# Four projections by seven block products, their weight sums begun at the split of the input, copies on SyncE's queue

## The chip, the core and the metric

The kernel runs on one core of a Trainium2 chip. A core has four compute engines and a fifth that only issues transfers, each with its own instruction queue: TensorE (PE, matrix products into an accumulator memory, PSUM), VectorE (DVE), ScalarE (ACT), GpSimd (POOL) and SyncE (SP). SyncE and GpSimd begin DMA transfers, which 16 DMA engines carry out. An engine runs its instructions in the order in which they are written and waits, at each, for the semaphores that the instruction names.

The metric is the device time of one execution, in microseconds, as the median of several runs; lower is better.

## What is computed

One layer of a hybrid block on 512 rows of width 1024, with 16 learned rows ahead of them (528 in all). Cut to what matters here:

```python
u  = rmsnorm(h)
c_in, q, k, v, z, a_dt, b_beta, gate_logits = split(u @ w_in)

c = c_val * sigmoid(c_gate)                    # 1024 wide
c = causal_dwconv(c, conf_dw_w)                # 31 taps
c = silu(layernorm(c))
y_conf = c @ w_conf_out                        # 1024 x 1024

qkv = silu(causal_dwconv([q, k, v], dn_conv_w))   # 4 taps
o = chunk_gated_delta_rule(q, k, v, g, beta)   # 8 heads, chunks of 64, in order
o = rmsnorm(o) * silu(z)
y_dn = o @ w_dn_out                            # 1024 x 1024

h = h + (sigmoid(gA) * y_conf + sigmoid(gB) * y_dn) @ w_out   # 1024 x 1024
up = causal_dwconv(rmsnorm(h) @ w_up)          # 1024 x 5632
return h + (silu(f_gate) * f_val) @ w_down     # 2816 x 1024
```

and a last norm. Everything is float32.

## The kernel before

**Layout.** Activations are kept transposed, features on the 128 partitions and the 516 columns that are still needed (4 of the learned rows, 512 others) along the free dimension, in two halves of 258. A product of float32 accuracy is made of three products of reduced operands: each operand is split into a high part (`wh`, `uh`, `oh`, `ch`, `mh`, `nh`) and a low part (`wl`, `ul`, ...), and high x high, high x low and low x high are summed in PSUM. ScalarE makes a high part by a copy, VectorE the low part by a subtraction.

**A projection the plain way** (`gemm`): for one output tile of 128 features, one weight tile of 128 x 1024 is loaded by SyncE into `wr` (three buffers), split by `weights` into `wh` and `wl` (two buffers each), and 8 x 3 x 2 = 48 matmuls of 258 columns follow. The three matrices w_dn_out (wdn), w_conf_out (wco) and w_out (wo) are done so, eight output tiles each; in the trace the first two have the output `y`, the third `wo`. `gated` multiplies a result by its gate tile (`gt`); VectorE adds the two branches, and the high and low parts `mh`, `ml` of the sum go into wo.

**A projection in seven block products** (`quarters`, `seven`, `factors`): most of w_up is done for a pair of output tiles and the two column halves at once, as a product of 2 x 2 blocks in seven block products of twelve matmuls. Two PSUM tiles, `sx` and `sz`, take turns; a running accumulator is read out after each product (`use`). `factors` makes the sums and differences of the activations' blocks and splits them (`nh`, `nl` and `nhl`). The sums of the weights' blocks don't depend on the activations: `presums` forms them in HBM (tiles `ws`, 19 sets), by two plain copies and three accumulating DMAs a set, which are all issued by GpSimd, so the later ones of a set wait there for the earlier. `seven` then loads them (`wr<-ws`) like weights: three tiles and a half for a pair, where the plain way has two.

**The middle.** Before these products stand the input projection `w_in` (outputs cg, cv, q, k, v, z, ga), the 31-tap convolution on VectorE (`ca<-c`, one instruction a tap and tile), the layer norm (its sums over features are small matmuls `rs<-ca`), the short convolutions (`conv4`, outputs `cv`, with `ra` as a padded copy) and, head by head, the chunked recurrence (`grow`, `heads`, `outs`). GpSimd has the masks of the heads (an affine select on `E`), memsets of padding (`ra`, `LL`) and 32 small copies (`mn<-DU`).

**The order of the work.** The program is not written in the order of execution. A planner (`Plan`) notes every operation and then lists them for each engine by readiness, priced durations and priorities; the priorities are the program's order plus biases of named parts (the table BIAS, and LNP, IVP, UP, WP), and SWITCH and STAY weigh changes between kinds of matmul. `plan.after` gives an operation a predecessor in this order. All instructions are written out by one line, 469, so the trace names that line for each of them, and a reader goes by the names of tiles.

Of the kernel before, what the change touches and what calls it, by code (L numbers as in the profile page):

```python
# [11 lines left out]
F32 = mybir.dt.float32  # L12
F32R = mybir.dt.float32r
# [12 lines left out]
H = 8  # L26
# [204 lines left out]
class Plan:  # L231
# [66 lines left out]
    def price(self, eng, fn, a, k, out):  # L298
# [173 lines left out]
def record(A, out):  # L472
# [612 lines left out]
    def heads(h):  # L1085
# [8 lines left out]
        with plan.at(f"s{h}"):  # L1094
# [39 lines left out]
            for n in range(NC):  # L1134
# [18 lines left out]
                if n < NC - 1:  # L1153
                    s = s1
# [351 lines left out]
```

## Time and profile before

| | us |
|---|---|
| median of 3 runs | 1016.2 (1014.99 to 1018.35) |
| the profiled execution | 1018.73 |
| its span, first to last instruction | 1016.9 |
| TensorE busy | 995.6 (98%), 8202 instructions |
| VectorE busy | 766.4 (75%), 1304 |
| ScalarE busy | 526.2 (52%), 945 |
| GpSimd busy | 108.4 (11%), 172 |
| mean granted TensorE clock | 0.994 of the full one |

The profiled execution is one run, 2.5 us above the median. Shares of busy time are averages over the stages: the input projection with the heads (to about 500 us), y and then wo (to 650 us), w_up (to 882 us) and w_down. TensorE's matmuls overlap, so the mean duration of one in the trace is longer than the distance between two; the pace of a stage is its length over its count. A DMA's row in a queue gives its bytes and its share of the 16 engines' time.

### The profile page before, as it was taken

To read this page: it belongs to the slowest core of one execution; us is meant where nothing else is said; L and a number is where in the kernel's file an instruction comes from. 1 tells how busy PE (TensorE), PEld (TensorE's weight loads), DVE (VectorE), ACT (ScalarE), POOL (GpSimd) and SP (SyncE) were. 2 spreads that over 40 slices of the span, in tenths; PEclk is the share of its full clock that TensorE was granted. 3 is DMA by queue.
4 is the path that set the end of the run, shared out by engine and by line. 5 is a ranking of instruction groups with operands and counts; after the bars stand their busy time and mean duration, and the time that the engine had idled before them with its cause. 6 is when DMAs were issued, how large, how long until landed. Compare 5 with 4: busy or idle time off the path is not lost.

```text
span 1016.9 us, 20105 instructions
## 1 busy us (share of the span) xinstructions
PE 995.6 (98%) x8202; PEld 949.7 (93%) x8202; DVE 766.4 (75%) x1304; ACT 526.2 (52%) x945; POOL 108.4 (11%) x172
## 2 busy tenths in 40 slices
PE   9999999999999999999999999999999999999996
PEld 6999999999989998989999999999999999988886
DVE  5988959689979998989485455599998988832334
ACT  5688732263644554355373224467786766632222
POOL 0011221523421222120000000000000000000000
PEclk9999999999999999999999999999999999999998
DMA  6144698988688897883313244424555556643332
GB/s 224 63 124 97 174 208 218 254 161 191 178 152 203 217 221 158 206 195 87 123 63 110 98 167 138 133 84 145 176 179 184 189 164 185 206 136 101 99 93 83
DMA packets 67932, 157.39 MB, mean 155 GB/s; under 512 B 15104, under 2 KB 21632, under 8 KB 67840
## 3 DMA queue, kind: packets, MB, share of 16 engines
q1 hardware_dynamic: 51728, 116.26, 36.1%
q0 software_dynamic: 16112, 39.85, 20.4%
q8 instruction: 64, 1.05, 0.4%
q14 instruction: 28, 0.23, 0.1%
HBM read 150.78 MB, written 45.16 MB: 193 GB/s over the span
## 4 chain that ended last, share of the span: by engine, by line
PE 72%; DMA 12%; issue 6%; DVE 5%; ACT 3%; POOL 1%; SPq 0%; DVEq 0%; ACTq 0%; POOLq 0%
PE dn L469 12%; PE sx L469 10%; PE y L469 9%; DMA ws<-in_wuq 7%; PE sz L469 7%; PE wo L469 5%; PE cv L469 5%; PE ga L469 4%; PE cg L469 4%; PE up L469 3%; PE z L469 2%; PE v L469 2%; DMA ws<-ws 2%; DMA eg<-d_e 2%; PE q L469 2%
## 5 line engine op out<-in xcount | busy, mean ns | idle before, releaser
L469 DVE TENSOR_TENSOR wl<-wr,wh 128x1024 fp32r<-128x1024 f32 (+2 forms) x195 | 225.6, 1158 | 156.0 <-PE dn L469 61.6
L469 ACT CAST wh<-wr 128x1024 fp32r<-128x1024 f32 (+2 forms) x195 | 193.8, 996 | 222.0 <-PE dn L469 56.4
L469 DVE SCALAR_TENSOR_TENSOR ca<-c,par,ca 128x516 f32<-128x516 f32 (+10 forms) x240 | 178.4, 750 | 6.3 <-ACT ca L469 2.3
L469 DVE SCALAR_TENSOR_TENSOR uy<-up,par,uy 128x512 f32<-128x512 f32 x88 | 64.2, 746 | 1.8 <-ACT uy L469 1.4
L469 POOL DMA_DIRECT2D ws<-in_wuq x57 | 49.3, 872 | 151.3 <-DMA ws<-in_wuq 77.7
L469 PE MATMUL dn<-fh,wh 128*128 128x512 f32 (+1 forms) x171 | 61.8, 369 | 0.0
L469 PE MATMUL dn<-fl,wh 128*128 128x512 f32 (+1 forms) x171 | 61.8, 369 | 0.0
L469 PE MATMUL sx<-nh,wh 128*128 128x258 f32 x228 | 60.5, 289 | 1.2 <-ACT wh L469 0.9
L469 PE MATMUL sz<-nl,wh 128*128 128x258 f32 x228 | 59.8, 283 | 0.0
L469 PE MATMUL sx<-nl,wh 128*128 128x258 f32 x228 | 59.4, 282 | 0.0
L469 PE MATMUL sz<-nh,wh 128*128 128x258 f32 x228 | 59.4, 283 | 0.0
L469 PE MATMUL ga<-ul,wh 128*128 128x258 f32 (+1 forms) x256 | 59.0, 294 | 0.0
L469 PE MATMUL ga<-uh,wh 128*128 128x258 f32 (+1 forms) x256 | 58.7, 294 | 0.0
L469 DVE SCALAR_TENSOR_TENSOR cv<-ra,par,cv 128x528 f32<-128x528 f32 x69 | 50.8, 758 | 6.2 <-POOL ra L469 5.9
L469 PE MATMUL ga<-uh,wl 128*128 128x258 f32 (+1 forms) x256 | 48.4, 295 | 0.0
L469 POOL DMA_DIRECT2D ws<-ws x38 | 35.8, 951 | 93.6 <-DMA ws<-in_wuq 58.8
L469 PEld LDWEIGHTS sx<-nh,wh 128*128 128x128 f32 x228 | 43.1, 189 | 2.9 <-ACT wh L469 1.4
L469 PE MATMUL sz<-nh,wl 128*128 128x258 f32 x228 | 44.6, 283 | 0.0
L469 PEld LDWEIGHTS sx<-nl,wh 128*128 128x128 f32 x228 | 43.2, 190 | 0.0
L469 PEld LDWEIGHTS sz<-nh,wh 128*128 128x128 f32 x228 | 42.9, 189 | 0.1
L469 PEld LDWEIGHTS sz<-nl,wh 128*128 128x128 f32 x228 | 42.9, 189 | 0.0
L469 PEld LDWEIGHTS ga<-ul,wh 128*128 128x128 f32 x256 | 42.7, 192 | 0.3
(324 smaller groups left out, 2764.7 us busy)
## 6 DMA issues: line engine op xcount, KB each, us to landing
wr<-in_win SPq DMA_DIRECT2D x64, 512.0 KB
ws<-in_wuq POOLq DMA_DIRECT2D x57, 512.0 KB, 7.9
wr<-ws SPq DMA_DIRECT2D x38, 512.0 KB
ws<-ws POOLq DMA_DIRECT2D x38, 256.0 KB, 6.1
wr<-in_wuq SPq DMA_DIRECT2D x19, 512.0 KB
wr<-in_wd SPq DMA_DIRECT2D x17, 512.0 KB
wr<-in_wuq SPq DMA_DIRECT2D x19, 256.0 KB
wr<-in_wdn SPq DMA_DIRECT2D x8, 512.0 KB
```

The costliest lines, as they stand in the source:

```text
L469: getattr(engines[o.eng], o.fn)(*(get(x) for x in o.a), **{n: get(x) for n, x in o.k.items()})
```

## The change

The three projections wdn, wco and wo are put into the form that most of w_up has: `quarters` for wdn and wco, `seven` with its own `use` for wo, where VectorE adds all seven results into `x`. Their weights are packed accordingly (`_quarters`). `presums` makes 4 sets for each of the three beside the 19 of w_up, all held (in the planner's order) only by the last write of the split input. In `presums`, the two plain copies are issued by SyncE, the three accumulating DMAs by GpSimd as before. Memsets of `ra` and `LL` go from GpSimd to VectorE, the copies `mn<-DU` to ScalarE. The factors of the heads' outputs and of the convolution's are made in pairs of tiles. The planner's tables are other ones, and its price of a GpSimd transfer is raised.

```diff
-STAY = 3000
-SWITCH = 375
...
+STAY = 600
+SWITCH = 1875
...
-LNP = -146
+LNP = -1476
...
             if eng == "POOL":
-                return 1000, int(np.prod(out.shape)) * 4 / 140.0
+                return 1000, int(np.prod(out.shape)) * 4 / 122.0
...
     def presums(src, n, hold):
...
-            G.dma_start(out=r[m][:, 0:2], in_=src[:, m, 0:3:2])
+            SY.dma_start(out=r[m][:, 0:2], in_=src[:, m, 0:3:2])
             plan.after = set(h)
-            G.dma_start(out=r[m][:, 2:4], in_=src[:, m, 0:2])
+            SY.dma_start(out=r[m][:, 2:4], in_=src[:, m, 0:2])
             G.dma_start(out=r[m][:, 1:3], in_=src[:, m, 3:4].broadcast_to([P, 2, HD]), accum_op=ALU.add)
...
-    G.memset(a[:, :PAD], 0.0)
+    V.memset(a[:, :PAD], 0.0)
...
+    softs, done = [], max(j for _, j, w in uh[-1].tl.hist if w)
+    wds, wcs, wos = (presums(A[n], KT // 2, done) for n in ('wdn', 'wco', 'wo'))
+    wus = presums(A['wuq'], FT - NPRE, done)
...
-            G.memset(l[0:32, :, 32:64], 0.0)
+            V.memset(l[0:32, :, 32:64], 0.0)
...
-                G.tensor_copy(out=Mn[h][r, :, r], in_=D8(h)[r])
+                S.copy(out=Mn[h][r, :, r], in_=D8(h)[r])
...
-    wus = presums(A['wuq'], FT - NPRE, masks[-1])
...
-    def gated(t, wsrc, ah, al):
-        acc = p2("y")
-        gemm(acc, weights(wsrc), ah, al, MIDR)
-        V.scalar_tensor_tensor(out=halves(t[:, :TW], HW), in0=halves(t[:, :TW], HW), scalar=1.0, in1=acc[:, :, MID],
-                               op0=ALU.add, op1=ALU.mult)
-        return t
+    def gated(m, wsrc, sums, B, ts):
+        for c, t in zip(quarters(wsrc, m, sums, B, HW, "yc"), ts):
+            V.scalar_tensor_tensor(out=t[:, :TW], in0=t[:, :TW], scalar=1.0, in1=c[:, :TW], op0=ALU.add, op1=ALU.mult)
+        return ts
+    for h in range(1, H, 2):
+        with plan.at(f"f{h}"):
+            ob.append(factors(zs[h - 1], zs[h], HW, "o", vals[-1]))
...
+    for f in range(1, KT, 2):
+        with plan.at("ln"):
+            cb.append(factors(*cacc[f - 1:f + 1], HW, "c", dns[f // 2]))
+    mb = []
+    for m in range(KT // 2):
+        ys = call(lambda m: gated(m, A['wco'], wcs, cb, [gts[2 * m], gts[2 * m + 1]]), "c", m)
+        for i, y in enumerate(ys):
+            V.tensor_tensor(out=y[:, :TW], in0=y[:, :TW], in1=ydn[2 * m + i][:, :TW], op=ALU.add)
+        mb.append(factors(*ys, HW, "m"))
...
+        where = {'p1': (x0, 0, 0.5), 'c11b': (x0, 0, 0.5), 'u2': (x0, 1, 0.5), 'c12b': (x0, 1, 0.5),
+                 'u3': (x1, 1, -0.5), 'c22b': (x1, 1, -0.5), 'c21': (x1, 0, -0.5)}
+        def use(what, acc):
+            x, b, by = where[what]
+            xb = x[:, b * HW:(b + 1) * HW]
+            V.scalar_tensor_tensor(out=xb, in0=acc, scalar=by, in1=xb, op0=ALU.mult, op1=ALU.add)
+        seven(A['wo'], m, wos, mb, HW, use)
...
-    a['wco'], a['wdn'], a['wo'] = _pack(w_conf_out[0]), _pack(w_dn_out[0]), _pack(w_out[0])
+    a['wco'], a['wdn'], a['wo'] = _quarters(w_conf_out[0]), _quarters(w_dn_out[0]), _quarters(w_out[0])
```

**From c to wo.** TensorE's order before, from the last matmul of `y` on (`y_16` is the last tile of c, `mh_7`, `mh_4`, ... are the high parts of tiles of the branches' sum); the last tile's, `mh_8`, come after 28 matmuls of `wo_1`:

```order
L469 MATMUL y_16_7463<-ch_8_6843,wl_80_7420 128x260
L469 MATMUL wo_1_7536<-mh_7_7494,wh_81_7439 128x258
L469 MATMUL wo_1_7536<-mh_7_7494,wh_81_7439 128x260
L469 MATMUL wo_1_7536<-ml_7_7502,wh_81_7439 128x258
L469 MATMUL wo_1_7536<-ml_7_7502,wh_81_7439 128x260
L469 MATMUL wo_1_7536<-mh_4_7309,wh_81_7439 128x258
L469 MATMUL wo_1_7536<-mh_4_7309,wh_81_7439 128x260
L469 MATMUL wo_1_7536<-ml_4_7316,wh_81_7439 128x258
L469 MATMUL wo_1_7536<-ml_4_7316,wh_81_7439 128x260
```

and after, from the last matmul of c on (`sx_8` its accumulator, `sx_9` and `sz_9` those of wo's first pair; `mh_10`, `mh_11` and `ml_10`, `ml_11` are factors made of the last pair of c, `mh_4` and `mh_5` of the first):

```order
L469 MATMUL sx_8_7624<-chl_4_7157,wl_96_7742 128x258
L469 MATMUL sx_9_7804<-mh_5_7523,wh_97_7787 128x258
L469 MATMUL sx_9_7804<-ml_5_7537,wh_97_7787 128x258
L469 MATMUL sz_9_7808<-mh_4_7517,wh_97_7787 128x258
L469 MATMUL sz_9_7808<-ml_4_7526,wh_97_7787 128x258
L469 MATMUL sz_9_7808<-mh_10_7821,wh_97_7787 128x258
L469 MATMUL sx_9_7804<-mh_11_7828,wh_97_7787 128x258
L469 MATMUL sz_9_7808<-ml_10_7830,wh_97_7787 128x258
L469 MATMUL sz_9_7808<-mh_1_7402,wh_97_7787 128x258
L469 MATMUL sz_9_7808<-ml_1_7432,wh_97_7787 128x258
L469 MATMUL sz_9_7808<-mh_7_7722,wh_97_7787 128x258
L469 MATMUL sx_9_7804<-ml_11_7838,wh_97_7787 128x258
```

The first seven rows that follow c's last hold three that need the last pair's factors. VectorE's order at the same place before (`y_16` gated, the branches added, the low part of the last tile `ml_8`):

```order
L469 TENSOR_TENSOR wl_82_7538<-wr_82_7385,wh_82_7513 128x1024
L469 SCALAR_TENSOR_TENSOR gt_8_5440<-gt_8_5440,y_16_7463 128x516
L469 TENSOR_TENSOR gt_8_5440<-gt_8_5440,gt_5_4314 128x516
L469 TENSOR_TENSOR ml_8_7575<-gt_8_5440,mh_8_7568 128x516
L469 TENSOR_TENSOR wl_83_7607<-wr_83_7434,wh_83_7589 128x1024
L469 SCALAR_TENSOR_TENSOR xr_1_7446<-wo_1_7536,xr_1_7446 128x516
```

and after (`yc_16` is the last tile of c; `wl_97` the low part of the weights of wo's first tile):

```order
L469 TENSOR_TENSOR gt_1_2042<-gt_1_2042,gt_9_5309 128x516
L469 SCALAR_TENSOR_TENSOR gt_15_6669<-gt_15_6669,yc_16_7739 128x516
L469 TENSOR_TENSOR mt_4_7816<-gt_1_2042 128x258
L469 TENSOR_TENSOR gt_15_6669<-gt_15_6669,gt_16_6679 128x516
L469 TENSOR_TENSOR wl_97_7819<-wr_97_7703,wh_97_7787 128x1024
L469 TENSOR_TENSOR gt_1_2042<-gt_15_6669,gt_1_2042 128x258
L469 SCALAR_TENSOR_TENSOR mt_4_7816<-mt_4_7816,gt_15_6669 128x258
L469 TENSOR_TENSOR ml_10_7830<-gt_15_6669,mh_10_7821 128x2x258
L469 SCALAR_TENSOR_TENSOR mq_4_7835<-mt_4_7816,gt_15_6669 128x258
L469 TENSOR_TENSOR ml_11_7838<-gt_1_2042,mh_11_7828 128x2x258
```

The low part of a weight tile and four half-width operations now stand among the steps from c's last result to `ml_11`.

**The layer norm's sums.** TensorE's order before, around the sums over features (`rs_4<-ca`), which follow the last gate tile (`ga_16`):

```order
L469 MATMUL ga_16_6320<-uh_8_125,wl_64_6328 128x258
L469 MATMUL ga_16_6320<-uh_8_125,wl_64_6328 128x260
L469 MATMUL rs_4_6388<-ca_8_5753,ones_1_65 32x129 x4
...
L469 MATMUL rs_4_6388<-ca_1_1181,ones_1_65 32x129 x4
L469 MATMUL z_15_6427<-uh_1_87,wh_65_6372 128x258
L469 MATMUL z_15_6427<-uh_1_87,wh_65_6372 128x260
```

and after, where they stand between a head's products (`qk_8`, `qkm_8`) while gate tile `ga_10` and `z_9` are in work:

```order
L469 MATMUL ga_10_5631<-ul_7_135,wh_54_5471 128x258
L469 MATMUL qk_8_5731<-cv_32_5647,cv_10_1552 128x128 x4
L469 MATMUL rs_3_5736<-ca_8_5065,ones_1_86 32x129 x4
...
L469 MATMUL rs_3_5736<-ca_1_1101,ones_1_86 32x129 x4
L469 MATMUL qkm_8_5770<-cv_32_5647,cv_10_1552 16x16
L469 MATMUL kS_29_5772<-S_29_5724,cv_10_1552 128x128
```

Ahead of these sums there are 3,730 matmuls in the order before and 3,240 after.

**SyncE's queue in c.** Before, c's weights (`in_wco`) are loaded one after another:

```order
L469 DMA wr_73_6880<-in_wdn 128x1024
L469 DMA wr_74_6899<-in_wco 128x1024
L469 DMA wr_75_6943<-in_wco 128x1024
L469 DMA wr_76_7028<-in_wco 128x1024
L469 DMA wr_77_7060<-in_wco 128x1024
L469 DMA wr_78_7141<-in_wco 128x1024
L469 DMA wr_79_7172<-in_wco 128x1024
```

After, loads of block sums (`ws_5`, `ws_8`) stand among them, and the two plain copies of the last set of w_up (`ws_31<-in_wuq`):

```order
L469 DMA wr_85_7282<-in_wco 128x1024
L469 DMA wr_86_7318<-ws_5_1660 128x1024
L469 DMA wr_87_7325<-ws_5_1660 128x1024
L469 DMA wr_88_7381<-in_wco 128x512
L469 DMA ws_31_7412<-in_wuq 128x2x512
L469 DMA wr_89_7423<-in_wco 128x1024
L469 DMA wr_90_7458<-ws_8_2103 128x1024
L469 DMA wr_91_7467<-ws_8_2103 128x1024
L469 DMA xr_1_7481<-in_xT 128x516
L469 DMA xr_2_7484<-in_xT 128x516
L469 DMA ws_31_7412<-in_wuq 128x1024
L469 DMA wr_92_7559<-in_wco 128x1024
```

The queue now changes between weights, ready sums and copies whose results are read only by w_up.

## Rows read from the trace of the kernel before

**Rows 1.** The page: busy time, share of the span and instructions of each engine.

```profile
PE 995.6 (98%) x8202; PEld 949.7 (93%) x8202; DVE 766.4 (75%) x1304; ACT 526.2 (52%) x945; POOL 108.4 (11%) x172
```

**Rows 2.** Windows: from:to, length, busy us (count) of PE, PEld, DVE, ACT, POOL, clock, DMA.

```profile
0.00:100.00 100.00, 96.99 (x771) 87.49 (x772) 78.44 (x190) 71.95 (x161) 7.57 (x23) 1.00 0.42 129
100.00:430.00 330.00, 323.99 (x2990) 314.86 (x2990) 285.48 (x532) 157.86 (x328) 94.19 (x141) 0.99 0.83 194
430.00:500.00 70.00, 68.04 (x580) 65.99 (x578) 59.67 (x89) 32.43 (x63) 6.64 (x8) 1.00 0.56 147
500.00:603.00 103.00, 102.99 (x946) 101.94 (x945) 56.26 (x74) 42.64 (x59) 0.00 (x0) 1.00 0.28 94
...
690.00:882.00 192.00, 190.64 (x1561) 188.44 (x1561) 176.41 (x256) 140.35 (x228) 0.00 (x0) 1.00 0.58 179
```

**Rows 3.** Chain of waits: start us, us, what.

```profile
524.53 66.01 PE y L469 x547
...
602.70 46.55 PE wo L469 x384
...
735.38 1.45 PE sz L469 x12
```

**Rows 4.** Groups by form, VectorE: out<-in, count | busy us, mean ns | idle before.

```profile
L469 DVE TENSOR_TENSOR wl<-wr,wh 128x1024 fp32r<-128x1024 f32 x168 | 204.9, 1221 | 133.2 <-PE dn L469 49.8 <-ACT wh L469 32.0 <-PE y L469 15.8
...
L469 DVE TENSOR_TENSOR wl<-wr,wh 128x512 fp32r<-128x512 f32 x19 | 13.0, 687 | 7.2 <-PE sz L469 3.4 <-ACT wh L469 2.0 <-ACT up L469 1.7
...
L469 DVE TENSOR_TENSOR up<-up,sx 128x258 f32<-128x258 f32 x19 | 7.9, 416 | 0.0
```

**Rows 5.** Timeline of VectorE from 602.3 us: start us, us, what.

```profile
602.79 1.23 DVE L469 TENSOR_TENSOR wl<-wr,wh 128x1024 fp32r<-128x1024 f32 x1 [1.70 <-PE y L469]
603.94 0.68 DVE L469 SCALAR_TENSOR_TENSOR gt<-gt,y 128x516 f32<-128x516 f32 x1
604.65 0.70 DVE L469 TENSOR_TENSOR gt<-gt,gt 128x516 f32<-128x516 f32 x1
606.04 0.70 DVE L469 TENSOR_TENSOR ml<-gt,mh 128x516 fp32r<-128x516 f32 x1 [0.69 <-ACT mh L469]
```

**Rows 6.** Timeline of ScalarE from 602.3 us.

```profile
605.38 0.62 ACT L469 CAST mh<-gt 128x516 fp32r<-128x516 f32 x1 [3.50 <-DVE gt L469]
```

**Rows 7.** Groups by form, ScalarE.

```profile
L469 ACT ACTIVATE up<-sx 128x258 f32<-128x258 f32 x19 | 7.2, 377 | 0.0
```

**Rows 8.** Tile ws: least/median/most ns, first and last start.

```profile
L469 POOL DMA_DIRECT2D ws<-in_wuq x57: 533/872/1352, 113.8 to 449.1; - x57
```

**Rows 9.** DMA queues and issues, 150 to 450 us.

```profile
q0 software_dynamic: 13949, 34.77, 59.6%
q1 hardware_dynamic: 11792, 24.61, 24.9%
...
ws<-ws POOLq DMA_DIRECT2D x32, 256.0 KB, 6.4
```

**Rows 10.** DMA queues, 700 to 860 us.

```profile
q1 hardware_dynamic: 8892, 28.18, 56.8%
```

**Rows 11.** Groups by form, GpSimd.

```profile
L469 POOL DMA_DIRECT2D ws<-in_wuq x57 | 49.3, 872 | 151.3 <-DMA ws<-in_wuq 77.7 <-issue 73.7
...
L469 POOL COPY mn<-DU 32x128 f32<-32x128 f32 x32 | 18.9, 596 | 2.8 <-DMA DU<-d_x 1.6
```

**Rows 12.** Timeline of TensorE at 500 us.

```profile
500.13 1.97 PE L469 MATMUL rs<-ca,ones 128*32 128x129 f32 x64
```

**Rows 13.** Tile ca, 430 to 500 us.

```profile
L469 DVE SCALAR_TENSOR_TENSOR ca<-c,par,ca x40: 642/746/757, 429.8 to 484.0; 128x516 f32<-128x516 f32 x12, 128x507 f32<-128x507 f32 x2, 128x506 f32<-128x506 f32 x2, 128x505 f32<-128x505 f32 x2
```

**Rows 14.** Waits: engine, line <- waited for: us in total, times, longest.

```profile
POOL E L469 <- DMA E<-d_g: 99.8, 4, 71.6
...
DVE cv L469 <- POOL ra L469: 5.9, 3, 2.8
...
PE vp L469 <- ACT cv L469: 4.7, 3, 2.4
```

More of the change, by code (lines that the diff above doesn't have):

```diff
@@ L162 @@
+LNP = -1476
+IVP = 730
+UP = 7189
+WP = 44
 WARM = 16
@@ L853, in conv4 @@
                 a = bt(n="ra")
-                G.memset(a[:, :PAD], 0.0)
+                V.memset(a[:, :PAD], 0.0)
                 S.copy(out=halves(a[:, PAD:], 264), in_=acc[:, :, :264])
@@ L941, in grams @@
             SY.dma_start(out=d_m[b, h].rearrange("n j t -> j n t"), in_=mn[32 * b:32 * b + 32, :, 32 * b:32 * b + 32])
-    masks, softs = [], []
+    masks = []
     ivt = {}
@@ L1078, in glu @@
                     taps.append(len(plan.ops) - 1)
-    oh, ol = [], []
+    ob, zs, vals = [], [], []
     d_r = con([H, T], "d_r", "dram")
@@ L1154, in heads @@
                     s = s1
+            vals.append(len(plan.ops) - 1)
             o2 = bt(n="o2")
@@ L1189, in outs @@
             V.tensor_tensor(out=z[:, :TW], in0=z[:, :TW], in1=rb[:, :TW], op=ALU.mult)
-            a, b = split(z[:, :TW], TW, "o")
-            oh.append(a)
-            ol.append(b)
+            zs.append(z)
     def call(fn, name, i):
@@ L1231, in record @@
             gts[i] = call(gate, "t", i)
-    def gated(t, wsrc, ah, al):
-        acc = p2("y")
-        gemm(acc, weights(wsrc), ah, al, MIDR)
-        V.scalar_tensor_tensor(out=halves(t[:, :TW], HW), in0=halves(t[:, :TW], HW), scalar=1.0, in1=acc[:, :, MID],
-                               op0=ALU.add, op1=ALU.mult)
-        return t
-    chh, chl = [], []
+    def gated(m, wsrc, sums, B, ts):
[5 more added lines that the diff above has]
+            ob.append(factors(zs[h - 1], zs[h], HW, "o", vals[-1]))
+    cb = []
     def layer_norm():
@@ L1257, in layer_norm @@
             S.activation(out=cacc[f][:, :TW], in_=cacc[f][:, :TW], func=AF.Silu, scale=pc('lw', f), bias=pc('lb', f))
-            a, b = split(cacc[f][:, :TW], TW, "c")
-            chh.append(a)
-            chl.append(b)
     with plan.at(LNP), plan.at("ln"):
         layer_norm()
-    ydn = [call(lambda f: gated(gts[KT + f], A['wdn'][f], oh, ol), "y", f) for f in range(KT)]
-    mh, ml = [], []
-    for f in range(KT):
-        y = call(lambda f: gated(gts[f], A['wco'][f], chh, chl), "c", f)
-        V.tensor_tensor(out=y[:, :TW], in0=y[:, :TW], in1=ydn[f][:, :TW], op=ALU.add)
-        a, b = split(y[:, :TW], TW, "m")
-        mh.append(a)
-        ml.append(b)
+    ydn, dns = [], []
@@ new lines, in record @@
+    for m in range(KT // 2):
+        ydn += call(lambda m: gated(m, A['wdn'], wds, ob, [gts[KT + 2 * m], gts[KT + 2 * m + 1]]), "y", m)
+        dns.append(max(i for i, o in enumerate(plan.ops) if o.eng == "PE"))
+    dns = [vals[-1]] + dns[1:2] + dns[1:3]
+    for f in range(1, KT, 2):
+        with plan.at("ln"):
+            cb.append(factors(*cacc[f - 1:f + 1], HW, "c", dns[f // 2]))
+    mb = []
+    for m in range(KT // 2):
+        ys = call(lambda m: gated(m, A['wco'], wcs, cb, [gts[2 * m], gts[2 * m + 1]]), "c", m)
+        for i, y in enumerate(ys):
+            V.tensor_tensor(out=y[:, :TW], in0=y[:, :TW], in1=ydn[2 * m + i][:, :TW], op=ALU.add)
+        mb.append(factors(*ys, HW, "m"))
@@ L1276, in record @@
     HS = 2
     hs, hh, hl, sq = [], [], [], []
[L1278 to L1296 removed]
+    for m in range(KT // 2):
+        for f in (2 * m, 2 * m + 1):
+            x = bt(n="xr")
+            SY.dma_start(out=x[:, :TW], in_=A['xT'][f][:, T0:T])
+            hs.append(x)
+        x0, x1 = hs[2 * m:]
+        where = {'p1': (x0, 0, 0.5), 'c11b': (x0, 0, 0.5), 'u2': (x0, 1, 0.5), 'c12b': (x0, 1, 0.5),
[5 more added lines that the diff above has]
+        seven(A['wo'], m, wos, mb, HW, use)
+        for f in (2 * m, 2 * m + 1):
+            x = hs[f]
+            hi, lo = bt(F32R, "hh"), bt(F32R, "hl")
+            S.mul(out=hi[:, HS:HS + TW], in_=x[:, :TW], mul=pc('nf', f))
+            V.scalar_tensor_tensor(out=lo[:, HS:HS + TW], in0=x[:, :TW], scalar=pc('nf', f), in1=hi.bitcast(F32)[:, HS:HS + TW],
+                                   op0=ALU.mult, op1=ALU.subtract)
+            hh.append(hi)
+            hl.append(lo)
+            s = bt(n="hsq")
+            S.activation(out=s[:, :TW], in_=x[:, :TW], func=AF.Square)
+            if f:
+                V.tensor_tensor(out=s[:, :TW], in0=s[:, :TW], in1=sq[:, :TW], op=ALU.add)
+            sq = s
```

24 lines of the change are left out of this document (1 added, 23 removed).

## The prediction

> **What bounds the kernel now.** Read the page's first part, then the windows by stage, then the chain of waits. The page: TensorE is busy 995.6 of 1016.9 us, VectorE 75%, ScalarE 52%, GpSimd 11% [rows 1]. The average hides the stages [rows 2]. From 100 to 430 us VectorE is at 285.5 of 330 us (87%) beside a nearly full TensorE; from 500 to 603 us, where w_dn and w_co are multiplied (tile y), TensorE has no idle time and VectorE is at 55%; from 690 to 882 us, where w_up already runs in seven products, TensorE is still at 99% but VectorE at 176.4 of 192 us (92%). So TensorE is the bound everywhere, and a seven-product stage has nearly used up VectorE. In the chain, w_o is 46.55 us of unbroken matmuls, the longest piece of y 66.01 us, and one product of w_up (12 matmuls) 1.45 us [rows 3]. That gives 46.55/384 = 0.121 us a matmul, in either form.
>
> **What it removes.** Per pair of output tiles, 96 matmuls become 7 x 12 = 84. There are 4 pairs in each of w_dn, w_co and w_o: 1152 matmuls become 1008. 144 x 0.121 = 17.4 us of TensorE, all in stages where it never waits. This is the term -17.4, if TensorE stays without waits there.
>
> **What it adds on VectorE, in y and c.** A pair loads 3.5 weight tiles for 2, each with a subtraction of 1.22 us (0.69 at half size), adds three block results of 0.42 us [rows 4], and forms the block factors: five half-width operations at the same price and three of about 0.70 us. In VectorE's order, 125 operations stand from the first addition of a block result of y to the gating of the last tile of c: 22 x 1.22 + 8 x 0.69 (weights) + 24 x 0.42 (results) + 30 x 0.42 (half-width parts of the factors) + 18 x 0.70 (their low parts) + 23 x 0.69 (gating and the sum of y and c) = 83.3 us, with the low part's 0.70 and the gating's 0.68 and 0.70 from the end of c [rows 5]. TensorE's work from the first result to the last product is 648 x 0.121 = 78 us. So VectorE needs about 5 us more than TensorE there, even with no gap; at the 92% that it reached from 690 to 882 us it would need 90.5 us, 12 more. On the other side, successive starts lie some 0.08 us closer than a weight subtraction's length (602.79 + 1.23 against 603.94) [rows 5], which gives back 2 us of the 5. I take +4, bounds 0 and 12. For w_o the same count gives 4 x (4.35 for weights + 7 x 0.42 for results + 4 x 0.70 for what the next norm and w_up need) = 40.4 us beside 40.5 of TensorE; each of its seven results must leave the accumulator within the 1.45 us of the other accumulator's product, with a subtraction of 1.22 us often ahead in the queue. +1, bounds 0 and 4. ScalarE's additions (24 casts of weights, 32 results, 24 casts of factors, 32 copies that were GpSimd's; at 0.3 to 1 us some 50) lie on an engine at 41% of the stage from 500 to 603 us [rows 2]: nothing.
>
> **The passage from c to w_o.** Before, the first output tile of w_o has 28 matmuls (3.4 us) on seven factors that are ready while the last one is made: product 0.68, sum 0.70, cast 0.62, low part 0.70 us [rows 5, 6], and the chain shows no wait [rows 3]. After, four matmuls of w_o use ready factors, then mh_10, mh_11 and ml_10 of the last pair are asked for, three more ready ones follow, and the eleventh waits for ml_11. After TensorE's last product of c: result copied 0.38 [rows 7], gating 0.68, half-width part 0.42, sum 0.70, then the weight subtraction of 1.22 that stands in VectorE's order, two half-width parts 0.84, first low part 0.70, half-width part 0.42, second low part 0.70: 6.1 us. TensorE has 10 matmuls (1.2 us) to put against it: +4.9, taken as +5, bounds 3 and 7. From w_o to w_up the chain is short against 24 ready matmuls, 2.9 us: nothing.
>
> **The block sums.** Before, 19 sets take from 113.8 to past 449.1 us: 335/18 = 18.6 us a set [rows 8], and nothing of them lies beside y, c and w_o. Now there are 31 sets. Begun at the split, near 80 us, at the same pace they last until 80 + 31 x 18.6 = 657 us; with two copies of a set no longer behind GpSimd's waits, less. In SyncE's order the copies of the last five sets stand among the weight loads of y and c. While sums run, they take 59.6% of the 16 DMA engines, beside 24.9% for loads [rows 9]; a seven-product stage by itself takes 56.8% [rows 10]. Together 116% is asked in y and c, which lasts 81 us: if loads yielded in proportion, 0.16 x 81 = 13 us of waits. But the sums aren't due until w_up and can slip, while three tile buffers let loads run ahead, and the pairs of sets leave gaps. Bounds 0 and 13; I take +2.5, nearer the low end, since 84.5% beside TensorE cost no visible wait. The copies themselves wait for no engine, and what is queued behind them on SyncE is weight loads, each held back by an issue; a GpSimd issue is 872 ns [rows 11], so two at most 1.7 us, hidden by the buffers.
>
> The Trainium skill, DMA: Bandwidth & Descriptors, section "Issuing engines are not separate DMA queues", says that DMAs begun by different engines end up on the same 16 DMA engines and interleave, and that issuing from several saves only sequencer time. By that rule the move to SyncE's queue takes no load off; the trace agrees as far as both queues' shares are of the same 16 engines [rows 9]. The sum stays as it is; the rule's own outcome is the rival on loads below.
>
> **The first stretch.** The layer norm's sums stand at 500 us now [rows 12]; in the new order some 490 matmuls fewer precede them, which is where TensorE of before stood near 430 us. VectorE must then have done by 430 us what it did later for the norm: the 40 taps of 0.75 us that began between 429.8 and 484.0 us [rows 13], 30 us, and of the other 30 us of that window [rows 2] what stands ahead of the sums in the new order, a few short convolutions and the 27 small memsets that were GpSimd's: I count 36 us in all, against 330 - 285.5 = 44.5 us of idle time before 430. That is 97% full. At 92% (the fullest stage seen) it would be 19 us late; with work moved to the first 100 us, or other work put off, nothing. TensorE's order is fixed, so lateness is a wait. +2, bounds -3 and 16. Against this, waits on GpSimd go: VectorE waited 5.9 us for its memset (ra), and TensorE 4.7 us for ScalarE's end of the same convolutions [rows 14]; the 32 copies of 596 ns [rows 11] leave a queue in which they stood behind DMA waits. -2, bounds 0 and -5.
>
> **Sum.** -17.4 + 4 + 1 + 5 + 2.5 + 2 - 2 = -4.9 us. The profiled execution took 1018.73 us (span 1016.9 and 1.8 around it), which gives 1013.8; the median of the runs is 1016.2, 2.5 lower, so the forecast is 1011.
>
> **Rivals.** 1. All covered: VectorE keeps up and loads are in time; only the passage from c to w_o is paid. -17.4 + 3 + 1 - 2 = -15.4: 1001. For it: TensorE ran at 99% beside a VectorE at 92%. Against it: the 83 us beside 78.
> 2. VectorE packed before the layer norm: TensorE waits at the norm's sums for taps. With 10 us there for the 2 of the forecast: 1019. For it: the 97%. Against it: VectorE was idle for another 21.6 of the first 100 us [rows 2], into which a new order may move work.
> 3. The slower side: loads late in y and c. The mechanism is the shared 16 engines: all of the 116% falls on the loads, 13 us for the 2.5 of the forecast. 1011 + 10.5 = 1021.5. Without that term the sum is -7.4, so from waits of 7.4 us on nothing of the gain is left, and from 10.5 on the change is measurably slower. For it: five sets beside y and c where there were none; against it: sums may slip.
> 4. GpSimd does not become free: three accumulating DMAs of each set, 93 in all (95 issues before), stay in its queue, each waiting for a transfer of 6.4 us or more [rows 9], and the masks behind them. GpSimd's mask waits were 99.8 us [rows 14]; if the last masks come late for their heads, the -2 becomes +1: 1014.
>
> **Chances.** Forecast 0.45 (its own range 1004 to 1017), all covered 0.20, packed before the norm 0.15, loads late 0.14, GpSimd not free 0.06. This kernel's measurement can tell about 0.3%, 3.05 us, from no change: faster is under 1013.15, slower over 1019.25. Faster: 0.30 + 0.20 + 0.02 + 0 + 0.04 = 0.56. Same: 0.14 + 0.06 + 0.03 + 0.01 = 0.24. Slower: 0.01 + 0.07 + 0.11 + 0.01 = 0.20. The range takes in the first rival and the third to its price: 999 to 1022.
>
> **What would show it.** TensorE's count down by 144 matmuls, and y, c and w_o together near 122 us of busy time; in the window from the first to the last result of y and c VectorE above 95% and TensorE waiting there for VectorE's low parts (wl), not for DMA; one wait of 4 to 6 us at w_o's first products, for ml or mh; hardware and software queues together above 90% in y and c. Waits of TensorE that go back through ScalarE's casts to DMA wr would show the third rival, a wait at rs the second. It is wrong if y, c and w_o stay without waits, or if more than 10 us are lost in one place.

## The result: slower by 3.1%

The changed kernel takes 1047.5 us (median of 4, 1042.7 to 1052.9) where the kernel before takes 1015.6 (median of 4, 1014.2 to 1018.4). The ratio is 1.031, with a 95% interval of 1.026 to 1.037. The forecast was 1011, its range 999 to 1022: wrong in sign and outside the range. The profiled execution of the changed kernel is the slowest of its four, 1052.9 us, 5.4 above the median; that of the kernel before took 1018.7, 3.1 above. So the rows show some 2 us more of loss than the medians.

The page's first part, against [rows 1]: span, then busy time of each engine; below it the clock and DMA lines of its forty slices.

```profile
span 1051.1 us, 20227 instructions
...
PE 995.3 (95%) x8058; PEld 944.9 (90%) x8058; DVE 823.2 (78%) x1471; ACT 576.9 (55%) x1060; POOL 94.2 (9%) x111
...
PEclk9998899999899999899999998999999999999999
DMA  6286799989888889769989987633555655644332
```

TensorE has 144 matmuls fewer, as forecast, and the same busy time: what the products gave is taken up by matmuls at a lower clock (mean granted 0.978, before 0.994), and the span is 34 us longer with TensorE idle. Stretch by stage, columns as in [rows 2]; y and c run here from 530 to 634 us, w_o to 685:

```profile
0.00:100.00 100.00, 91.32 (x718) 84.31 (x719) 71.53 (x171) 65.03 (x127) 9.00 (x20) 0.97 0.59 169
100.00:430.00 330.00, 314.32 (x2856) 301.85 (x2855) 293.80 (x581) 167.89 (x378) 55.01 (x59) 0.97 0.88 205
...
530.00:634.00 104.00, 88.69 (x681) 85.22 (x679) 76.44 (x124) 51.75 (x89) 14.27 (x15) 0.97 0.89 228
634.00:685.00 51.00, 43.89 (x336) 42.53 (x336) 40.34 (x68) 24.62 (x35) 0.00 (x0) 0.93 0.68 219
...
720.00:918.00 198.00, 197.12 (x1611) 194.99 (x1611) 185.00 (x272) 144.99 (x235) 0.00 (x0) 1.00 0.58 178
```

Before 430 us TensorE is idle for 24 us, where it was for 9 [rows 2]. In y and c TensorE is busy 88.7 of 104 us, and the DMA engines are busy 89% of the time, instead of 28%. From 720 us on, where w_up runs, nothing is lost. From the chain of waits in y and c, its transfers alone (start, length, what); in the kernel before the chain had only matmuls there [rows 3]:

```profile
535.35 9.09 DMA wr<-ws
...
546.87 6.57 DMA wr<-in_wdn
...
554.92 7.18 DMA wr<-in_wdn
...
576.83 8.04 DMA wr<-ws
...
587.31 8.07 DMA wr<-ws
...
598.43 9.09 DMA wr<-in_wco
...
615.74 8.61 DMA wr<-ws
...
629.46 7.31 DMA wr<-ws
```

Loads of weights and of block sums end last, 7 to 9 us each. What TensorE waited for from 525 to 690 us: engine, tile, releaser, us in total, times, longest.

```profile
PE sx L469 <- ACT wh L469: 7.1, 5, 4.3
PE sx L469 <- ACT yc L469: 6.2, 4, 2.7
PE sz L469 <- ACT mh L469: 4.2, 1, 4.2
PE sx L469 <- DVE xr L469: 2.7, 3, 1.4
```

These lines name the engine that came last. In the chain, a load of weights or sums stands one step back from a cast `wh`, and two steps back from a result `yc` that ScalarE copies after that cast. The wait for `mh` is the passage from c to w_o: 4.2 us where the forecast had 5.

The early loss, in 10 us windows:

```profile
80.00:90.00 10.00, 4.08 (x27) 3.87 (x26) 3.89 (x13) 3.15 (x7) 0.81 (x1) 0.84 0.68 151
90.00:100.00 10.00, 9.83 (x66) 9.37 (x66) 8.04 (x14) 7.72 (x26) 3.33 (x5) 0.82 0.73 202
120.00:130.00 10.00, 6.28 (x34) 5.98 (x35) 7.07 (x16) 8.50 (x26) 2.71 (x4) 0.66 0.85 160
```

From 80 to 90 us TensorE works 4.1 of 10 us. Its granted clock is 0.82 in the ten us behind that wait and 0.66 around the one near 120, a mixture of its two levels of 2.4 and 1.2 GHz. GpSimd's timeline there:

```profile
77.95 0.81 POOL L469 DMA_DIRECT2D ws<-ws  x1 [5.71 <-DMA ws<-in_wdn]
82.12 0.81 POOL L469 DMA_DIRECT2D ws<-ws  x1 [3.35 <-DMA ws<-ws]
91.81 0.84 POOL L469 DMA_DIRECT2D ws<-ws  x1 [8.88 <-DMA ws<-ws]
92.44 2.70 POOL L469 TENSOR_SCALAR_AFFINE_SELECT E<-E 128x512 f32<-128x512 f32 x4
```

and of the kernel before:

```profile
72.99 3.94 POOL L469 TENSOR_SCALAR_AFFINE_SELECT E<-E 128x512 f32<-128x512 f32 x4 [71.56 <-DMA E<-d_g]
```

The first four masks (E) stand behind three waits for block sums and come 19 us later. At the same time a transfer of 8 KB that a head needs (`Em`) takes 11.7 us to land. (Without accumulating DMAs, in x_no_acc below, it is issued at 73.2 and its first reader runs at 77.9.) Behind it a plain copy of a set (`ws<-in_wdn`) is the next long transfer in the chain:

```profile
73.00 11.74 DMA Em<-d_gm
...
97.88 7.90 DMA ws<-in_wdn
```

### The profile page after: what moved, and what is told of

Read it like the earlier page. It is cut to its first block, busy times and chain, and to the rows that moved or that the text cites. A ratio compares the mean times of both kernels' runs of the same rounds, so it can differ in the third digit from the quotient of the medians.

```text
span 1051.1 us, 20227 instructions
## 1 busy us (share of the span) xinstructions
PE 995.3 (95%) x8058; PEld 944.9 (90%) x8058; DVE 823.2 (78%) x1471; ACT 576.9 (55%) x1060; POOL 94.2 (9%) x111
## 3 DMA queue, kind: packets, MB, share of 16 engines
q0 software_dynamic: 17360, 32.51, 21.8%
## 4 chain that ended last, share of the span: by engine, by line
PE 61%; DMA 13%; DVE 13%; ACT 3%; issue 2%; SPq 1%; POOL 0%; ACTq 0%; DVEq 0%
PE sx L469 12%; PE dn L469 12%; PE sz L469 9%; PE ga L469 6%; DVE wl L469 4%; DVE ca L469 4%; DMA wr<-ws 4%; PE q L469 3%; PE up L469 3%; PE v L469 3%; PE z L469 3%; ACT wh L469 2%; DMA orb<-d_r 2%; PE o L469 1%; DMA wr<-in_wdn 1%
## 5 line engine op out<-in xcount | busy, mean ns | idle before, releaser
L469 ACT CAST wh<-wr 128x1024 fp32r<-128x1024 f32 (+2 forms) x219 | 213.9, 977 | 239.7 <-PE dn L469 52.5
L469 DVE TENSOR_TENSOR wl<-wr,wh 128x1024 fp32r<-128x1024 f32 (+2 forms) x219 | 249.5, 1141 | 116.3 <-PE dn L469 61.2
L469 DVE SCALAR_TENSOR_TENSOR ca<-c,par,ca 128x516 f32<-128x516 f32 (+11 forms) x240 | 177.1, 746 | 3.4 <-ACT ca L469 1.2
L469 POOL DMA_DIRECT2D ws<-ws x62 | 59.1, 953 | 190.4 <-DMA ws<-ws 87.5
L469 DVE SCALAR_TENSOR_TENSOR uy<-up,par,uy 128x512 f32<-128x512 f32 x88 | 63.8, 747 | 1.4 <-ACT uy L469 1.2
L469 PEld LDWEIGHTS ga<-uh,wh 128*128 128x128 f32 x256 | 42.8, 189 | 0.4 <-issue 0.2
```

The costliest lines, as they stand in the source:

```text
L469: getattr(engines[o.eng], o.fn)(*(get(x) for x in o.a), **{n: get(x) for n, x in o.k.items()})
```

## The experiments

Theory A: the transfers of the sums take the DMA engines from weight loads and from the heads' small transfers. Theory B: VectorE's added work and the new order cost the time, without the transfers. Names with x_ are the changed kernel with one edit, names with b_ the kernel before with one or a few, and y7 is a step between the two. All edits but those of y7 and y7_ns are made where instructions are written out, so the order of everything else stays as it is. The code is cut to the lines that matter. In the table, "y begins" is TensorE's first product of y in the profiled run (where y is plain and mixed with other work: the first product of w_o less 768 x 0.1205 us, so the 92.5 of these kernels is set and not measured), then the length from there to w_o's first product and from that to the first seven-product of w_up.

| kernel | us | ratio to before (95%) | y begins | y and c | to w_up |
|---|---|---|---|---|---|
| before | 1015.6 | 1 | 510.0 | 92.5 | 82.7 |
| changed | 1047.5 | 1.031 (1.026 to 1.037) | 530.4 | 103.2 | 87.6 |
| x_no_sums | 1014.3 | 0.998 (0.996 to 1.000) | 504.2 | 91.7 | 87.2 |
| x_no_acc | 1014.8 | 0.996 (0.993 to 0.998) | 503.8 | 91.1 | 87.2 |
| x_no_late | 1036.6 | 1.021 (1.016 to 1.026) | 522.4 | 91.7 | 87.3 |
| x_no_early | 1033.3 | 1.018 (1.014 to 1.022) | 507.6 | 103.2 | 88.6 |
| x_early_no_acc | 1035.5 | 1.016 (1.011 to 1.021) | 506.6 | 105.0 | 87.4 |
| x_acc_behind | 1042.3 | 1.027 (1.022 to 1.031) | 517.5 | 102.4 | 88.4 |
| x_moved | 1049.5 | 1.032 (1.027 to 1.036) | 523.0 | 90.6 | 87.9 |
| x_copies_pool | 1043.3 | 1.026 (1.022 to 1.030) | 526.2 | 101.2 | 87.9 |
| x_ns_lean | 1008.6 | 0.989 (0.987 to 0.991) | 504.5 | 88.5 | 84.2 |
| b_ns | 1005.5 | 0.989 (0.985 to 0.992) | 497.2 | 92.5 | 82.7 |
| y7 | 1035.2 | 1.014 (1.009 to 1.018) | | | 82.2 |
| y7_ns | 1014.2 | 0.996 (0.995 to 0.998) | | | 82.2 |
| b_masks_only | 1012.7 | 0.995 (0.993 to 0.997) | 502.2 | 92.5 | 82.7 |
| b_spread | 1014.5 | 0.996 (0.994 to 0.998) | 506.0 | 92.5 | 82.7 |

The kernels were timed on several chips (before took 1015.5 to 1020.2 us on them), so the ratio is what to compare. The last three columns are of one profiled run each. Where accumulating DMAs run, such a run can lie 3 to 5 us off its median (x_no_late 3.7 and x_early_no_acc 4.3 below, x_copies_pool 4.3 above), so a difference of that size in "y begins" says little there.

**All sums left out** (x_no_sums).

```diff
+                m, step = part(i)
+                if m in SKIP:
+                    continue
...
+                    k['in_'] = w
```

Here `m` is the set (0 to 30), `step` the transfer of it (0 to 4) and SKIP is `range(31)`; the last line lets a load of a set that is left out read plain weights.

> The changed kernel in its own order, with all 155 transfers of the 31 sets of block sums left out; the tiles that held sums are read from the plain weights instead, so loads, casts and products are the same in number and size and the values are wrong. Theory A (the sums take the DMA engines from the weight loads and from the small transfers of the heads): the lost 32 us and more go, 1047 becomes 1000 to 1010, TensorE's clock is above 0.99 again, and y, c and w_o together take 122 to 132 us. Theory B (VectorE's added work and the new order of the work, not transfers, cost the time): at least 20 us of the loss stay, 1030 or more, with TensorE waiting for low parts of weights while loads lie ready.

The loss of 33 us goes: theory A for the loss. But 1014 isn't 1000 to 1010: without one transfer of sums the change is as slow as before, so theory B has a share that the 17.4 us of products pay for. Nor do the stages come out as expected: y, c and w_o together take 142.6 us, not 122 to 132 (504.2 to 646.8). Two windows of this kernel, and one of its 5 us slices:

```profile
504.00:596.00 92.00, 86.06 (x676) 84.24 (x676) 75.39 (x124) 51.50 (x88) 0.00 (x0) 0.96 0.53 166
596.00:647.00 51.00, 43.90 (x339) 42.44 (x338) 40.70 (x68) 24.95 (x35) 0.00 (x0) 0.97 0.64 208
```

```profile
570.00:575.00 5.00, 2.04 (x16) 1.84 (x15) 4.97 (x10) 3.17 (x6) 0.00 (x0) 0.87 0.04 15
575.00:580.00 5.00, 5.00 (x25) 5.00 (x25) 2.62 (x3) 1.55 (x3) 0.00 (x0) 0.50 0.65 179
```

y and c last 91.7 us for 81 of products, and w_o 10 us more than its 40.5. From 570 to 575 us TensorE works 2.0 us and VectorE 4.97 of 5, with hardly a load under way; after that the clock is at 0.50, the lower level. What TensorE waits for in this kernel:

```profile
PE sx L484 <- DVE wl L484: 3.3, 2, 3.0
PE sz L484 <- ACT mh L484: 3.1, 1, 3.1
PE sx L484 <- ACT wh L484: 2.9, 3, 1.4
PE sx L484 <- DVE xr L484: 2.7, 3, 1.4
```

Low parts (`wl`), high parts (`wh`, ScalarE's), results that VectorE must take out of the accumulator (`xr`), factors (`mh`): in the main VectorE or what hangs on it.

**VectorE relieved** (x_ns_lean), without sums.

```diff
+                    nm = (k['out'].tl.name, k['in0'].tl.name, k['in1'].tl.name)
+                    if nm in (("gt", "gt", "gt"), ("hsq", "hsq", "hsq")) and k['out'].n == TW:
+                        continue
```

> As the kernel without any sums (1014.3), and with 15 additions of VectorE left out that no other engine waits for at once: the eight of the two branches (5.6 us, in c) and the seven of the squares for the next norm (4.8 us, in w_o). If VectorE bounds c and w_o, the stretch from y's first product to w_o's first falls from 91.7 to 85 to 88 us and that from w_o's first to the norm's products from 87 to 82 to 84: 1003 to 1007 in all. If the passage between stages and the order bound them, under 3 us go in all: 1011 or more.

10.4 us of VectorE's work less (8 sums of branches, 7 of squares) gives 6 us: 1014.3 to 1008.6, and 6.2 between the spans of the profiled runs, of which y and c have 3.2 and w_o 2.9. (The ratios, 0.998 and 0.989, would give 9, but they come from two chips.) The clock in y and c, 0.96 without the edit, is back at 1.00. So VectorE is part of what bounds c and w_o. Both stretches, and the whole, end a little above the expected ranges, so what else holds these stages, the passages and the order, isn't separated here.

**The last five sets, the first four** (x_no_late, x_no_early): the same edit with `range(26, 31)` and `range(0, 4)`.

> The changed kernel in its own order without the transfers of the last five sets (26 to 30 of 0 to 30), those whose copies stand among the loads of y and c; these five are read from plain weights. Theory A: the waits of y, c and w_o shrink by most of their 28 us, the stretch before y stays some 20 us late: 1047 becomes 1022 to 1032. Theory B: under 5 us change.

> The changed kernel in its own order without the first four sets (those of w_dn, begun at the input's split, done by about 140 us); they are read from plain weights. Theory A: the waits between 70 and 150 us go (6 us for the learned rows' small transfer, some 9 us for masks and what follows them, and the half clock after them): 8 to 16 us less, 1031 to 1039, and the loss from 500 us on stays. Theory B (the order itself makes the first stretch late): under 4 us change.

Each takes away its own stretch's loss (at the median 10.6 and 13.9 us, by the ratios). Without the last five sets, y and c take 91.7 us, as without any: 11.5 us for five sets. Without the first four, y begins at 507.6 instead of 530.4 and y and c stay at 103.2. x_no_early is where it was expected; x_no_late lies above its range, since y and c gained less than the 28 us that were expected of five sets.

**Which transfers of the first four** (x_early_no_acc): the copies kept, the accumulating DMAs out.

```diff
+                if 0 <= m < 4 and step >= 2:
+                    continue
```

> The changed kernel in its own order; of the first four sets (w_dn) the eight plain copies on SyncE's queue are kept and the twelve accumulating DMAs on GpSimd left out (values of these sums wrong). If the early loss of 14 us comes from masks that wait in GpSimd's queue behind accumulating DMAs, nearly all of it goes: 1032 to 1036. If it comes from the copies' load on the DMA engines and their places in SyncE's queue ahead of the heads' small transfers, half or more of it stays: 1038 to 1046.

All of the early loss goes (1.016, and 1.018 without the first four sets altogether), so it is the accumulating DMAs'; the eight copies by themselves cost nothing that can be seen. Whether it is GpSimd's queue or the load was asked by putting them **behind the last mask** (x_acc_behind):

```diff
+            late = [i for i in order[:last] if 0 <= part(i)[0] < 4 and part(i)[1] >= 2]
+            order = [i for i in order[:last + 1] if i not in late] + late + order[last + 1:]
```

> The changed kernel, whole, with one edit in GpSimd's queue: the twelve accumulating DMAs of the first four sets are issued behind the last mask instead of between the masks; their copies stay where they are. If masks that queue behind accumulating DMAs cause the early loss, or the accumulating DMAs' load on the heads' small transfers, y begins some 20 us earlier than in the changed kernel and most of 14 us is kept: 1033 to 1038. If what is put off collides with what comes later, the gain is given back by 500 us: 1042 to 1050.

5 us less, at the edge of the second expectation, with an interval (1.022 to 1.031) that overlaps the changed kernel's. The first masks come at 78.2 us instead of 92.4, but y begins at 517.5, 11 us later than in x_early_no_acc, where these DMAs are left out: the load that was put off costs later. **Moving sums** (x_moved) points the same way.

```diff
+            spot = {order[p]: last + (p - early[0]) * (early[-1] - last) / (early[-1] - early[0]) for p in early}
...
+                if m >= 26:
+                    spot[order[p]] = 7000 + 350 * (m - 26) + 70 * s
```

The first line moves the first 26 sets behind the last mask, the last one puts the other five among w_up.

> The changed kernel, whole, with the transfers of the sums at other places of the queues: the first 26 sets begin after the last mask and are closer together (84% of their spacing), the last five are spread over w_up. Theory A: most of the gains of leaving out the early and the late ones together, 25 us, less what the denser stretch costs: 1022 to 1032. If the load itself costs wherever it lies, 1038 or more.

No gain at all: y and c are as short as without late sets, but y begins at 523.0, 13 us later than in the kernel before, and in w_up TensorE is idle for 10 us, waiting in part for results (`sx<-up`, 5.1 us). In this kernel the load costs at each of the places that were tried.

**The copies back on GpSimd** (x_copies_pool): `e = "POOL"` for both copies.

> The changed kernel in its own order, but the two plain copies of each set are issued by GpSimd again, as before the change. If the queue of the copies is what delays loads (copies ahead of loads in SyncE's queue), the time falls by 10 us or more. If only the 16 DMA engines count, it stays within 6 us of 1047, or rises where GpSimd's masks wait behind more transfers.

Within 6 us of the changed kernel: which queue issues the copies hardly matters. The Trainium skill, DMA: Bandwidth & Descriptors, section "Issuing engines are not separate DMA queues", says that DMAs begun by different engines run on the same 16 DMA engines, and that only sequencer time is saved; this run agrees (1043.3 against 1047.5, intervals that overlap).

**All accumulating DMAs out, all copies kept** (x_no_acc): `if step >= 2: continue` for every set.

> The changed kernel in its own order with the 62 plain copies kept on SyncE's queue and all 93 accumulating DMAs left out (sums wrong). By count of bytes the copies are half of a set's transfers: if bytes count, half of the 33 us stays, 1028 to 1034 (ratio 1.013 to 1.018). If the accumulating ones carry the cost, as in the early stretch, under 10 us stay: 1015 to 1024 (ratio under 1.009).

This settles it: 1014.8, just under the lowest that was expected, and as fast as with no transfer at all (0.996 and 0.998). The 62 copies (32.5 MB) alone cost nothing that can be measured; all 33 us come with the 93 accumulating DMAs (32.5 MB). From 150 to 450 us, queues and loads of the changed kernel:

```profile
q0 software_dynamic: 9989, 18.72, 44.7%
q1 hardware_dynamic: 18211, 40.74, 42.6%
...
wr<-in_win SPq DMA_DIRECT2D x38, 512.0 KB, 6.1
```

and of x_no_acc:

```profile
q1 hardware_dynamic: 18909, 42.34, 44.5%
...
wr<-in_win SPq DMA_DIRECT2D x38, 512.0 KB, 3.4
```

18.7 MB of accumulating transfers hold the 16 engines for 44.7% of 300 us, 7.2 us a MB; 42 MB of plain ones for 44.5%, 3.2 us a MB. And with the accumulating ones in flight a load of 512 KB lands after 6.1 us instead of 3.4.

That accumulating DMAs are also the only ones in the software queue (GpSimd's) is a rival that x_copies_pool settles: there the copies are in it too. The software queue over the whole run, in the changed kernel and in x_copies_pool:

```profile
q0 software_dynamic: 17360, 32.51, 21.8%
```

```profile
q0 software_dynamic: 26288, 65.02, 31.4%
```

With 32.5 MB of copies more, the queue takes 31.4% of 1046 us instead of 21.8% of 1051: 3.1 us a MB, as in SyncE's queue. It is the accumulation that is dear, not the queue.

**What sums cost before** (b_ns): the 19 sets left out of the kernel before.

> The kernel before in its own order, with the transfers of its 19 sets left out (w_up reads plain weights in their place, values wrong). What sums cost already before: if they were hidden behind TensorE, under 3 us (1012 to 1016 where before has 1015); if each set costs about a microsecond as in the changed kernel, 8 to 20 us less.

They cost 1.1%, 11.6 us, as the second expectation had it, though no wait in [rows 14] names their transfers. A set's 0.6 us stands against the 1.45 us that a pair gains; with 31 sets the cost is 33 us, above 1 us a set.

This run also allows a comparison of like with like. Without any sums the changed kernel stands at 0.998 and the kernel before at 0.989: the change is some 9 us slower by itself (8.5 between the spans of the profiled runs; 7 with x_no_acc, timed on the chip of b_ns, in place of x_no_sums), and dearer sums, 33 us instead of 11.6, make up the other 22 of the 32 us lost.

**Only w_dn in seven products** (y7, and y7_ns without its 23 sets): `gated` by `quarters` for w_dn alone, in the planner's order that results.

> The kernel before with only w_dn in seven products: 4 more sets of sums (23), all issued by GpSimd and begun after the masks as before, 48 matmuls fewer (5.8 us). VectorE has 7 us of work for 10.1 of TensorE in that stage, and w_dn is followed by plain w_co, so neither the passage nor VectorE should cost. Theory A: the 23 sets last some 75 us longer, into y and c, where loads then ask for 0.57 and 0.28 of the DMA engines: 1009 to 1016. If the planner's order around the middle changes for the worse, 1016 to 1025.

> The kernel with only w_dn in seven products (1.4% slower than before), in its own order, without the transfers of its 23 sets. Theory A (transfers): it falls below before, by the 5.8 us that 48 matmuls are worth and a few that sums cost before: ratio 0.985 to 0.995. If its order of the work is what made it slow: ratio above 1.0.

The 23 sets cost 18 us between the two (1.014 to 0.996), where 19 cost 11.6 before. Without sums the order is still 8 us worse than that of b_ns (0.996 to 0.989), in spite of the 48 matmuls. Neither expectation was met: y7 is above both of its ranges, y7_ns just above the first one. In the profiled runs nearly all of the 18 us lies before y begins (504.2 and 486.3); the plain c takes 66.4 us in both.

**GpSimd freed, alone** (b_masks_only): the kernel before, with memsets of `ra` and `LL` on VectorE and the copies of `mn` on ScalarE.

```diff
+                if e == "POOL" and fn == "memset" and k_out(o) in ("ra", "LL"):
+                    e = "DVE"
+                if e == "POOL" and fn == "tensor_copy" and k_out(o) == "mn":
+                    e, fn = "ACT", "copy"
```

> The kernel before in its own order, with one part of the change alone: the memsets of ra and LL on VectorE and the 32 copies of mn on ScalarE, so that GpSimd has masks and the sums' DMAs only. The forecast's -2 (0 to -5): VectorE's 5.9 us of waits for ra go. If that was hidden or the added work takes as much, 0.

0.995 (0.993 to 0.997), some 5 us: the end of the forecast's range, and a version that beats both kernels, by little but clear of the noise. TensorE's wait for the convolutions' end shrinks from 4.7 us [rows 14]:

```profile
PE vp L490 <- ACT cv L490: 2.6, 2, 1.7
```

**Spreading the 19 sets** (b_spread), with that edit and the copies on SyncE:

```diff
+            spot = {order[p]: at[0] + (p - at[0]) * (read[0] - 150 - at[0]) / (at[-1] - at[0]) for p in at}
...
+                if m >= 0 and step < 2:
+                    e = "SP"
```

> The kernel before with three edits: memsets and copies away from GpSimd (ratio 0.9948 alone), the copies of the 19 sets issued by SyncE, and the sets spread from 114 to about 650 us instead of 461. If density costs, 3 to 8 us less than with the first edit alone: ratio 0.987 to 0.992. If each transfer costs wherever it lies, 0.993 to 0.997; if copies in SyncE's queue delay loads, above 0.998.

0.996, no better than without spreading. But this is not because each transfer costs wherever it lies. Four of the sets now run beside plain c and w_o; these two stages in this kernel, and in the kernel before, without sums there:

```profile
534.70:598.50 63.80, 63.80 (x530) 63.63 (x529) 30.68 (x37) 16.48 (x19) 7.35 (x8) 1.00 0.74 180
598.50:645.10 46.60, 46.60 (x387) 46.52 (x386) 24.98 (x31) 17.76 (x23) 3.68 (x4) 1.00 0.81 226
```

```profile
538.70:602.50 63.80, 63.79 (x530) 63.62 (x529) 30.70 (x37) 16.52 (x19) 0.00 (x0) 1.00 0.32 108
602.50:649.10 46.60, 46.60 (x387) 46.52 (x386) 24.97 (x31) 17.77 (x23) 0.00 (x0) 1.00 0.53 165
```

The DMA engines are busy 74% and 81% instead of 32% and 53%, and TensorE loses nothing: the same lengths, no idle time, clock 1.00. In the seven-product y and c of the changed kernel five sets cost 11.5 us. So the cost hangs on what runs beside: there a pair loads 3.5 weight tiles instead of two, and VectorE has 76.4 us of work in the 104, where it has 30.7 in the 63.8 of plain c; which of the two makes the difference was not tried. What b_spread loses against b_masks_only lies earlier (c begins at 534.7 instead of 530.9); why fewer sets in the first stretch gained nothing there is open.

## Why the prediction was wrong

**Two steps failed, the price of the block sums first.** It was taken as +2.5 us over the kernel before, in y and c only, bounded by 13 from shares of engine time there. Measured: the sums cost 33 us (x_no_sums, x_no_acc) where they had cost 11.6 (b_ns), so 22 more. In the profiled runs, of which the changed kernel's is 5 us above its median, 11.5 lie in y and c (x_no_late; close to the bound and to the third rival's 13, whose sign, waits that go back through casts to loads, is in the chain) and 26 before y begins (530.4 against 504.2); the first four sets alone cost 14 us at the median. For the first stretch the forecast had no such term: it counted sets, pace and copies, and asked what ended last in SyncE's queue, but not what seven more sets beside the heads (26 instead of 19), whose first accumulating work is issued at 62.9 us where the first set began at 113.8, do to loads and to small transfers. [rows 9] held the warning: 34.8 MB in the software queue took 59.6%, 24.6 MB in the hardware queue 24.9%, so a MB there took 1.7 times as long, copies included. "84.5% cost no visible wait" was read from a page of the profile that names the last releaser only; b_ns shows that it cost 11.6 us. The fourth rival saw GpSimd's masks behind the sums, priced at 3 us. The masks do come 19 us late; taking the DMAs out of their way gains 5 us (x_acc_behind), taking them out altogether 15 (x_early_no_acc).

**The second step is the rest of the sum.** Without the 2.5 it is -7.4; like with like, without sums on either side, the change measures some +9 (x_no_sums against b_ns). VectorE and the passage to w_o were +4, +1 and +5, 10 us together; measured without sums, y, c and w_o take 21 us more than their products (10.7 and 10.4). The mechanism was right (x_ns_lean; the window with VectorE at 4.97 of 5), and the wait for `mh`, 4.2 us, near the 5 of the forecast. Too small were c, where VectorE's surplus doesn't spread over the stage but ends in two waits, and w_o, where results stay in the accumulator behind VectorE's other work. A lower clock behind the two longest waits, which the forecast didn't count, adds to it: in x_no_sums 0.50 from 575 to 580 us behind waits of 1.4 and 3.0 us, 0.63 from 600 to 604 behind one of 3.1, and 0.96 over the 92 us of y and c. In x_ns_lean, where the first two waits are 1.4 and 2.1 us, it stays at 1.00.

**The first stretch's order** was taken as +2 against -2 for GpSimd's waits. Without sums y begins at 504.2, 6 us earlier than before but 7 later than in b_ns. The second rival (packed before the norm) isn't the cause: the norm's sums run at 434.3 us in x_no_sums and at 460.5 in the changed kernel, and TensorE doesn't wait there in either. TensorE is idle for 7.6 us before 504 in x_no_sums and for 2.2 before 497 in b_ns; 3.0 of it lie between 100 and 150 us and 1.5 between 250 and 300, where b_ns has none. Which part of the new order makes these waits was not tried. GpSimd's relief is worth 5 us in the kernel before, where the sums keep its queue waiting; in b_ns the waits for `ra` are gone without it. So the terms for the first stretch, 0 together, are +7 when no sums run.

**What was right**: 144 matmuls fewer; nothing lost from w_up on; the copies on SyncE's queue cost nothing; from w_o to w_up no wait (TensorE busy 35.00 of 35 us from 685 to 720). The balance in profiled runs: y begins 20.4 us later, y and c take 10.7 more, w_o to w_up 4.9 more, the rest 1.8 less: 34.2, the difference of the spans.

Open: how much of an accumulating DMA's cost is the engines' time and how much the longer landing of everything beside it; what in it takes the engines twice a copy's time (the queue's rows count a byte once); why five sets cost 11.5 us beside seven products and four cost nothing beside plain ones; and why TensorE's part of the 33 us in the first stretch spreads over four places (80, 120, 260 and 420 us). It wasn't tried to form the sums in another way.

## What to carry to other kernels

Price a transfer by the time that it holds the DMA engines and by what it does to the landing of others, by kind, and not by bytes: here an accumulating DMA in HBM took over twice a copy's, and beside such DMAs loads landed in 6.1 us instead of 3.4. Ask, too, what runs beside it: such sums were free beside plain products of c and w_o and dear beside seven-product ones. Leave a suspected background stream out once, in the old kernel too: that a profile names no wait for it doesn't mean that it is free, and only the difference between the two kernels belongs to the change. When matmuls are saved at the cost of another engine's work, compare that engine's sum with TensorE's for the stage, and look at the granted clock behind each longer wait.

## What was not expected of the hardware

62 plain copies in HBM, 32.5 MB beside a busy TensorE, cost nothing measurable (0.996 against 0.998), and 93 accumulating DMAs of the same bytes 33 us. Yet four sets of them beside plain products cost TensorE nothing at 74% and 81% of the DMA engines (b_spread). And waits of 1.4 and 3.0 us close together were followed by a stretch at half clock (0.50 from 575 to 580 us in x_no_sums).
